# Hymba layer step: attention's value products in plain fp32, four heads to a PSUM bank

## Chip, cores and metric

The kernel runs on one core of a Trainium2 chip. The metric is device time in microseconds (us); lower is better. A core has five engines that each work through their instructions in order: TensorE (PE: matmuls, with weight loads, PEld, beside them), VectorE (DVE), ScalarE (ACT), GpSimd (POOL) and SyncE (SP), which here issues the DMAs. SBUF is the core's memory; PSUM's banks hold what PE writes.

## The reference, cut to what matters

One layer over a prompt of 512 tokens and 8 single sample tokens, `D_MODEL` 1024. The change concerns mixer B, dilated attention of 8 heads with 64 columns each, for the prompt:

```python
h = jnp.einsum('btd,de->bte', x, w_in)                      # 1024 -> 3600 columns
qa, ka, va, za, ga, qb, kb, vb, gb = jnp.split(h, split_points, axis=-1)
...                                                          # mixer A: gated linear attention -> o_a
# mixer B, for each (window, dilation) of (128,1), (512,4), (2048,16):
    logits = jnp.einsum('bqhd,bqjhd->bhqj', qf, kg) * scale + bias
    p = jnp.exp(logits - m);  s = jnp.sum(p, axis=-1, keepdims=True)
    outs.append(jnp.einsum('bhqj,bqjhd->bhqd', p, vg) / s)
out = (wts[0]*outs[0] + wts[1]*outs[1] + wts[2]*outs[2]) / (wts[0]+wts[1]+wts[2])
...
mix = jnp.concatenate([o_a * silu(ga), o_b * silu(gb)], axis=-1)
y = jnp.einsum('bte,ed->btd', mix, w_out)
x_new = layer_norm(DEEPNORM_ALPHA * x + y, ln_g, ln_b)
```

The keys and values of the prompt are outputs as well (`vw_p` in the kernel is the values' output, 512x512).

## The kernel before, in words

**Arithmetic.** All projections run in a reduced fp32 format (f32r) in three products: each operand is split into a high part, rounded to f32r by a cast, and a low part, the difference (`split`: a cast on ACT, a subtraction on DVE); then high by high, high by low and low by high are added in PSUM. Weights arrive by DMA in pieces (`raw0_gb0` is the first piece of group `gb0`), are split (`hi0_gb0`, `lo0_gb0`) and used by PE. The profile leaves the stage number out of such names: `hi_vb__1819` there is `hi1_vb1__1819` in the order of instructions.

**Who decides the order.** A small planner written in Python (`Plan`) runs while the program is built. Every piece of the layer is a generator, added with a priority (`add(weighted(h, pi), 30 + ...)`), that yields the next instruction, a need for a buffer, or a mark it waits for (`At`). The planner takes, again and again, the instruction that can start first by its own cost figures, and records it; on each engine the instructions then run in that order. A pair `copy(o, x)` may go to DVE or to ACT, whichever would end first by those figures; a `Batch` is recorded in one piece. Buffers come from pools with a fixed number of slots: `g` large SBUF tiles, `pt` probabilities, `t1` small temporaries, `ob` attention outputs, `r` raw weights; PSUM banks are of the kinds `d`, `s` and `t`. Since all instructions go out from one line of the planner, every line of the profile reads L359, and views go by the names of tiles.

**The stages on PE.** `dense` sets the sequence of the projections: `ka`, `za`, `qa`, `qb0` to `qb3`, `kb0` to `kb3`, `vb0`, `vb1`, `gb0` to `gb3`, `va0`, `va1`, `ga0` to `ga3`, then the output projection (`yf`, `y`) and the LayerNorm. All else is placed between their matmuls. The attention of the prompt runs in two halves `pi` of 256 queries: `scores` (two heads at a time, `ps_s`), `softmax` for each head and each tile of 128 queries, `weighted` for the product with the values, and `mix_b`, which multiplies by the gate. Beside it runs the attention of the samples over the cache: `past` and `qbc` come by DMA, POOL multiplies them, DVE reduces the product (`lt<-past`, eight times, named `past0` to `past7` in the order), and `l32` adds the samples' new key with a table `sel`.

**What the change touches.** `softmax` ends with a transpose on PE into a bank `ps_pt`, and from there a cast on ACT to the high part of the probabilities (`pt`, `pth`) and a subtraction on DVE to the low part (`pt`, `ptl`); one head of the first half has both parts in one slot, one of the second half takes two of the four. `vb_into` takes the values out of PSUM: for the first 256 tokens they come transposed and are turned back on PE (`ps_turn`), for the others they come in rows (`ps_vb`). Each piece is cast and subtracted into `vhl`, where a head's 64 high columns and 64 low ones stand side by side, and copied once more into a small tile (`raw` of `turn`, shown as `feat`, or `vb_raw`) from which a DMA stores it: eight stores of 128 KB. `weighted` multiplies for one head: the high probabilities by the 128 columns [high | low], the low ones by the 64 high columns:

```python
yield T.matmul(pv[:, o], vk, pth[:, k, o], start=k == 0, stop=False, ...)
yield T.matmul(pv[:64, o], vk[:, :64], ptl[:, k, o], start=False, stop=k == last, ...)
```

Partitions 64 to 127 of the bank are then copied by ACT (`pvl`, a slot of `t1`), and DVE adds the copy to partitions 0 to 63 into `obT`. These are 96 matmuls over both halves.

Of the kernel before, what the change touches and what calls it, by code (L numbers as in the profile page):

```python
# [11 lines left out]
F32 = mybir.dt.float32  # L12
# [46 lines left out]
    g=27,  # L59
# [304 lines left out]
def trunk(ctx: ExitStack, tc: tile.TileContext, xT, xp, xs, state, ck, cv, w_in, wab, gnorm,  # L364
# [44 lines left out]
    def copy(o, x):  # L409
        return V.tensor_copy(o, x), S.copy(o, x)  # L410
# [42 lines left out]
    class Group:  # L453
# [227 lines left out]
    def dense():  # L681
# [36 lines left out]
        for i in range(4):  # L718
            yield from make(f"kp{i}", Need("g", f"kp{i}", [P, 2, 512], F32R), 2)
            yield from feature(groups[f"kb{i}"], parts("k", k_s, i, 1.0))  # L720
        for i in range(2):
            for u in range(2):
                yield from make(f"vhl{i}{u}", Need("g", f"vhl{i}{u}", [P, 2, 4, 2, 64], F32R))
            yield from token(groups[f"vb{i}"], *vb_into(i))
# [343 lines left out]
    def vb_into(i):  # L1068
        def parts_of(o, x):
            yield S.copy(o[..., 0, :], x)  # L1070
            yield V.tensor_tensor(o[..., 1, :], x, o[..., 0, :].bitcast(F32), op=ALU.subtract)

        def evac_f(ps, f):
# [11 lines left out]
        def evac(ps, t):  # L1085
            yield from parts_of(B[f"vhl{i}1"][:, t - 2], ps.rearrange("p (h d) -> p h d", d=64))
            mark(f"vb{i}1")
            raw = yield Need("t1", "vb_raw", [P, GW])
            yield copy(raw, ps)
            free(ps)  # L1090
            yield D.dma_start(vw_p[t * P:t * P + P, i * GW:i * GW + GW], raw)
            free(raw)
        return evac_f, evac


# [46 lines left out]
    def softmax(h, q, ps_all, pr_all, cols):  # L1142
# [14 lines left out]
        if j == 0:  # L1157
            if pi:
                for x in "hl":
                    yield from make(f"pt{x}{h}{pi}", Need("pt", f"pt{x}{h}{pi}", [P, 4, 256], F32R))  # L1160
            else:
                B[f"pt{h}"] = yield Need("pt", f"pt{h}", [P, 2, 2, 256], F32R)
                B[f"pth{h}0"], B[f"ptl{h}0"] = B[f"pt{h}"][:, 0], B[f"pt{h}"][:, 1]
                mark(f"ptl{h}0")
        else:
            yield At(f"ptl{h}{pi}")
        pth, ptl = B[f"pth{h}{pi}"], B[f"ptl{h}{pi}"]
# [12 lines left out]
    def weighted(h, pi):  # L1180
        m, u = h // 2, (h % 2) * 64
        r = slice(u, u + 64)
        yield At(f"p{h}{pi}", 2)
        for i in range(pi + 1):
            yield At(f"vb{h // 4}{i}", 2)
        pth, ptl = B[f"pth{h}{pi}"], B[f"ptl{h}{pi}"]
        if h % 2 == 0:
            yield from make(f"obT{pi}{m}", Need("ob", f"obT{pi}{m}", [P, 256]))
        else:
            yield At(f"obT{pi}{m}")  # L1190
        pv = yield bank(("s", "t"), f"ps_pv{h}{pi}")
        last = 2 * pi + 1
        for k in range(last + 1):
            o = slice(P if k == last else 0, 256)
            vk = B[f"vhl{h // 4}{k // 2}"][:, k % 2, h % 4].rearrange("p u d -> p (u d)")
            yield T.matmul(pv[:, o], vk, pth[:, k, o], start=k == 0, stop=False, skip_group_check=True)
            yield T.matmul(pv[:64, o], vk[:, :64], ptl[:, k, o], start=False, stop=k == last, skip_group_check=True)
        free(*((pth, ptl) if pi else (pth,)))
        tmp = yield Need("t1", f"pvl{h}{pi}", [64, 256])
        yield S.copy(tmp, pv[64:, :256])  # L1200
        yield V.tensor_tensor(B[f"obT{pi}{m}"][r, :], pv[:64, :256], tmp, op=ALU.add)
        free(pv, tmp)
        mark(f"ob{pi}{m}")
        mark(f"ob{pi}")
        if B.setdefault(("pv_left", pi), 0) == HB - 1:
            if pi:
                free(*(B[f"vhl{i}{u}"] for i in range(2) for u in range(2)))
        B["pv_left", pi] += 1

# [173 lines left out]
    def mix_tiles(n, u):  # L1383
# [3 lines left out]
        else:  # L1387
            yield At(f"ob{u}0", 2)
# [23 lines left out]
    def mix_b(u, m):  # L1412
        yield At(f"ob{u}{m}", 2)
# [3 lines left out]
        yield V.tensor_tensor(gb, gb, B[f"obT{u}{m}"], op=ALU.mult)  # L1417
        free(B[f"obT{u}{m}"])
# [187 lines left out]
    add(keys_store(), 17.5)  # L1606
    for pi in range(2):
        for n in "ab":
            add(mix_tiles(n, pi), 13)
        for h in range(HB):  # L1610
# [3 lines left out]
            add(weighted(h, pi), 30 + 20 * pi / 100 + h / 100)  # L1614
# [100 lines left out]
```

## Time and profile before

| | |
|---|---|
| runs | 290.06, 289.52, 289.38 us; median 289.52 us |
| profiled execution, first to last instruction (span) | 286.8 us, 2.7 below the median of the runs; its own time outside the span is not recorded |
| granted TensorE clock | 0.994 |
| PE / weight loads | 275.0 us (96%) / 259.5 us (90%) |
| DVE / ACT / POOL | 225.7 us (79%) / 167.5 us (58%) / 55.9 us (19%) |
| DMA | 51.18 MB, mean 178 GB/s |
| value products on PE | first started at 104.5 us, last at 181.1 us, between `vb` and `va` |

Rows of groups give the line, the engine, the operation, the tile written and the tiles read, the shape, the count, the busy time with the mean of one, and behind the second bar the idle time of the engine just before, with what ended it. A row of the windows gives the length of the window and for PE, PEld, DVE, ACT and POOL the busy time with the number of instructions, then the granted clock, the share of the DMA engines' time and the rate. A row of the chain gives start, length and what ran; a row of the timeline adds in brackets the idle time before it and the releaser. Matmul ends are modelled; a matmul that waits inside the pipeline still counts as busy.

### The profile page before, as it was taken

Reading aid. Unit: us, or ns where it says so; the run is one execution under the profiler, and the core shown is the slowest. Engines: PE = TensorE matmul, PEld = TensorE weight load, DVE = VectorE, ACT = ScalarE, POOL = GpSimd, SP = SyncE. Lnnn points to the kernel's source line nnn. Section 1 sums busy time; section 2 is a strip of 40 time slices with the busy share of each in tenths; the row PEclk is TensorE's granted clock in tenths of the full one; section 3 lists DMA queues with packets and bytes.
Section 4 is the critical chain, followed back from the end, with each engine's and each line's share of the span. In section 5 each row is a group of like instructions: output and inputs, shape, how many; then the busy total and the mean of one; then the engine's idle time right before and its main releaser. Section 6 shows DMA issues by size and latency. Waiting matters only on the chain.

```text
span 286.8 us, 6896 instructions
## 1 busy us (share of the span) xinstructions
PE 275.0 (96%) x2636; PEld 259.5 (90%) x2636; DVE 225.7 (79%) x547; ACT 167.5 (58%) x478; POOL 55.9 (19%) x74
## 2 busy tenths in 40 slices
PE   8999999999999998999999999999999999999990
PEld 5899999998989998899989999999999999997880
DVE  3846897999889968988889997864888995339745
ACT  5757664554567777566869867526689774113201
POOL 4000001000782444401604444540000000000000
PEclk9999999999999999999999999999999999999997
DMA  7966522225866797648998987559754788741211
GB/s 209 269 191 195 147 75 75 75 78 167 296 201 222 196 287 230 175 130 243 274 201 188 239 227 219 149 149 228 221 95 148 230 297 252 111 151 73 78 75 73
DMA packets 58936, 51.18 MB, mean 178 GB/s; under 512 B 12555, under 2 KB 50197, under 8 KB 58903
## 3 DMA queue, kind: packets, MB, share of 16 engines
q1 hardware_dynamic: 58794, 50.66, 63.2%
q8 instruction: 21, 0.34, 0.5%
q14 instruction: 13, 0.10, 0.1%
q10 hardware_dynamic: 108, 0.07, 0.1%
HBM read 45.17 MB, written 6.03 MB: 179 GB/s over the span
## 4 chain that ended last, share of the span: by engine, by line
PE 71%; DVE 13%; DMA 8%; ACT 5%; issue 2%; SPq 1%; DVEq 0%; ACTq 0%
PE ps_qb L359 8%; PE ps_yf L359 8%; PE ps_y L359 8%; PE ps_ga L359 6%; PE ps_kb L359 4%; PE ps_qa L359 4%; PE ps_gb L359 4%; PE ps_va L359 4%; PE ps_ka L359 4%; DMA raw_gb__2152<-in_w_in_dram 3%; DMA out_dram<-feat 3%; PE ps_pt L359 2%; PE ps_va_f L359 2%; PE ps_l L359 2%; PE ps_s L359 2%; PE ps_pv L359 2%
## 5 line engine op out<-in xcount | busy, mean ns | idle before, releaser
L359 POOL TENSOR_TENSOR vv<-vv,pb 128x256 f32<-128x256 f32 x32 | 26.1, 846 | 45.5 <-DMA pb<-psd_s 39.8
L359 POOL TENSOR_TENSOR past<-past,qbc 128x256 f32<-128x256 f32 x32 | 25.6, 831 | 43.4 <-DMA past<-in_ck_dram 36.0
L359 ACT ACTIVATE pr<-pr,ms 128x128 f32<-128x128 f32 (+3 forms) x49 | 26.1, 546 | 5.8 <-DVE ms L359 5.2
L359 PE MATMUL ps_pt<-cf,pr 128*128 128x128 f32 x80 | 14.1, 280 | 1.4 <-DVE pt L359 1.0
L359 DVE CUSTOM_DVE_ANT_0 pr<-ps_s,strip 128x128 f32<-128x128 f32 (+3 forms) x32 | 14.3, 476 | 0.0
L359 PE MATMUL ps_ka<-xx,hi_ka 128*128 128x264 f32 (+1 forms) x64 | 13.5, 307 | 0.3 <-DVE xx L359 0.3
L359 ACT ACTIVATE sg<-sg 128x264 f32<-128x264 f32 (+1 forms) x32 | 13.4, 419 | 0.2
L359 PEld LDWEIGHTS ps_ka<-xx,hi_ka 128*128 128x128 f32 x64 | 11.0, 205 | 1.2 <-DVE xx L359 0.8
L359 DVE TENSOR_TENSOR ptl<-ps_pt,pth 128x384 fp32r<-128x384 f32 (+1 forms) x16 | 9.8, 617 | 2.8 <-ACT pth L359 2.8
L359 PEld LDWEIGHTS ps_pt<-cf,pr 128*128 128x128 f32 x80 | 9.0, 140 | 3.3 <-DVE pt L359 1.6
L359 ACT ACTIVATE d<-d 128x512 f32<-128x512 f32 x13 | 7.8, 637 | 6.7 <-DVE d L359 6.7
L359 ACT COPY feat_y<-ps_yf 128x256 f32<-128x256 f32 x8 | 3.0, 371 | 12.7 <-PE ps_yf L359 12.7
L359 ACT ACTIVATE rstd<-mv 128x1 f32<-128x1 f32 x4 | 0.7, 199 | 15.9 <-DVE mv L359 15.9
L359 POOL MEMSET att<- 64x512 f32 x2 | 1.0, 523 | 44.5 <-DVE ks L359 44.5
L359 ACT CAST pth<-ps_pt 128x384 fp32r<-128x384 f32 (+1 forms) x16 | 8.4, 534 | 2.2 <-PE ps_pt L359 2.0
L359 DVE TENSOR_REDUCE o_pv<-vv 128x4 f32<-128x1024 f32 x8 | 9.7, 1212 | 0.0
L359 DVE TENSOR_REDUCE lt<-past 128x16 f32<-128x1024 f32 x8 | 9.6, 1199 | 0.0
L359 PE MATMUL ps_ka<-xx,lo_ka 128*128 128x264 f32 (+1 forms) x32 | 9.4, 295 | 0.0
L359 DVE TENSOR_TENSOR obT<-ps_pv,pvl 64x256 f32<-64x256 f32 x16 | 6.6, 415 | 3.5 <-ACT pvl L359 3.3
L359 DVE TENSOR_TENSOR xx<-x_raw,xx 128x520 fp32r<-128x520 f32 (+2 forms) x9 | 5.8, 640 | 4.6 <-ACT xx L359 4.6
L359 ACT COPY pvl<-ps_pv 64x256 f32<-64x256 f32 x16 | 5.5, 370 | 6.1 <-PE ps_pv L359 5.3
L359 DVE TENSOR_TENSOR d<-b 128x1024 f32<-128x1024 f32 x7 | 8.5, 1218 | 0.0
(535 smaller groups left out, 1092.4 us busy)
## 6 DMA issues: line engine op xcount, KB each, us to landing
past<-in_ck_dram SPq DMA_DIRECT2D x8, 512.0 KB
vv<-in_cv_dram SPq DMA_DIRECT2D x8, 512.0 KB
pb<-psd_s SPq DMA_DIRECT2D x16, 256.0 KB
qbc<-qsd SPq DMA_DIRECT2D x8, 256.0 KB
strip<-tabr SPq DMA_DIRECT2D x8, 256.0 KB
y<-in_xp_dram SPq DMA_DIRECT2D x4, 512.0 KB
x_raw<-in_xT_dram SPq DMA_DIRECT2D x7, 260.0 KB
out_dram<-y SPq DMA_DIRECT2D x3, 512.0 KB
```

Of the source, the lines that this page charges most:

```text
L359: getattr(eng.eng, op.fn)(*op.args, **op.kw)
```

## The change

The probabilities and the values are no longer split. `softmax` copies the transposed probabilities once (DVE or ACT) as fp32. `vb_into` copies the values once, into two tiles `v0` and `v1` of 128 x 2 x 512 (two `g` slots instead of four, and `g` has 25 slots instead of 27), without the second copy; `values_store` stores each of the two tiles by one DMA of 512 KB when both column groups are in. `weighted` now works for a group of four heads: heads 0 and 2 of the group write partitions 0 to 63 of one bank, heads 1 and 3 partitions 64 to 127; heads 0 and 1 take the first 256 columns, 2 and 3 the last 256. Its plain fp32 matmuls, 8 for the first half of queries and 16 for the second (48 in all), are one batch in which the partition halves alternate, and one copy of 128x512 brings the bank to `obT`. It waits for the probabilities of all four heads, which hold the four `pt` slots until then.

```diff
-    g=27,
+    g=25,
...
-                tags += ("sv",) * (plan.marks["sample"] == 2) + ("pt",) * (plan.marks["ob1"] == HB) + ("g",)
+                tags += ("sv",) * (plan.marks["sample"] == 2) + ("pt",) * (plan.marks["ob1"] == 4) + ("g",)
...
     def vb_into(i):
-        def parts_of(o, x):
-            yield S.copy(o[..., 0, :], x)
-            yield V.tensor_tensor(o[..., 1, :], x, o[..., 0, :].bitcast(F32), op=ALU.subtract)
...
             ps, raw = yield from turn(ps)
-            yield from parts_of(B[f"vhl{i}0"][:, :, 2 * f:2 * f + 2], ps[:, :GW].rearrange("p (t h d) -> p t h d", t=2, d=64))
+            free(raw)
+            yield copy(B["v0"][:, :, c], ps[:, :GW].rearrange("p (t c) -> p t c", t=2))
+            free(ps)
             mark(f"vb{i}0")
-            yield copy(raw, ps[:, :GW])
+
+        def evac(ps, t):
+            yield copy(B["v1"][:, t - 2, i * GW:i * GW + GW], ps)
             free(ps)
-            yield D.dma_start(vw_p[:GW, c].rearrange("(t p) c -> p t c", p=P), raw.rearrange("p (t c) -> p t c", t=2))
-            free(raw)
...
+    def values_store(u):
+        for i in range(2):
+            yield At(f"vb{i}{u}", 2)
+        yield D.dma_start(vw_p[u * GW:u * GW + GW, :].rearrange("(t p) c -> p t c", p=P), B[f"v{u}"])
...
-        ptv = pt[:, :n].rearrange("p (k t) -> p k t", t=P)
-        yield S.copy(pth[:, :q + 1, qs], ptv)
-        yield V.tensor_tensor(ptl[:, :q + 1, qs], ptv, pth[:, :q + 1, qs].bitcast(F32), op=ALU.subtract)
+        yield copy(B[f"pt{h}{pi}"][:, :q + 1, qs], pt[:, :n].rearrange("p (k t) -> p k t", t=P))
...
-    def weighted(h, pi):
+    def weighted(g, pi):
+        hs = range(4 * g, 4 * g + 4)
+        for h in hs:
+            yield At(f"p{h}{pi}", 2)
+        for u in range(pi + 1):
+            yield At(f"vb{g}{u}", 2)
+        yield from make(f"obT{pi}{g}", Need("ob", f"obT{pi}{g}", [P, 2, 256]), 2)
+        pv = yield bank(("s", "t"), f"ps_pv{g}{pi}")
         last = 2 * pi + 1
+        pts = [B[f"pt{h}{pi}"] for h in hs]
+        every = [(k, h) for k in range(last + 1) for h in range(4)]
+        yield Batch(T.matmul(pv[h % 2 * 64:h % 2 * 64 + 64, h // 2 * GW + (P if k == last else 0):h // 2 * GW + GW],
+                             B[f"v{k // 2}"][:, k % 2, (4 * g + h) * 64:(4 * g + h) * 64 + 64], pts[h][:, k, P if k == last else 0:],
+                             start=k == 0 and h < 2, stop=k == last, skip_group_check=True) for k, h in every)
+        free(*pts)
+        yield copy(B[f"obT{pi}{g}"].rearrange("p m t -> p (m t)"), pv)
+        free(pv)
...
+    for u in range(2):
+        add(values_store(u), 17.5)
...
-            add(weighted(h, pi), 30 + 20 * pi / 100 + h / 100)
+            if h % 4 == 3:
+                add(weighted(h // 4, pi), 30 + 20 * pi / 100 + h / 100)
```

The planner is given other instructions and so records another order. Three places matter later; a name like `pt40` is head 4, query tile 0, and the number behind it is the buffer.

PE, at the first products, in the middle of the projection `vb0`; before, `ps_pv00` is head 0, half 0:

```order
L359 MATMUL ps_pv00_1727<-pt0_1262,vhl00_1578 128x256
L359 MATMUL ps_pv00_1727<-pt0_1262,vhl00_1578 64x256
L359 MATMUL ps_pv10_1728<-pt1_1294,vhl00_1578 128x256
L359 MATMUL ps_pv10_1728<-pt1_1294,vhl00_1578 64x256
L359 MATMUL ps_vb0_2_1679<-lo1_vb0__1408,xx6_240 128x256
L359 MATMUL ps_vb0_2_1679<-hi1_vb0__1407,xx6_241 128x256
L359 MATMUL ps_vb0_2_1679<-hi1_vb0__1407,xx6_240 128x256
L359 MATMUL ps_vb0_2_1679<-lo1_vb0__1408,xx6_240 128x256
L359 MATMUL ps_pv00_1727<-pt0_1262,vhl00_1578 128x128
L359 MATMUL ps_pv00_1727<-pt0_1262,vhl00_1578 64x128
```

The same place now; ten matmuls of `vb0` stand between the turning of the value tile and the first of these rows:

```order
L359 MATMUL ps_vb0_2_1672<-hi1_vb0__1403,xx6_240 128x256
L359 MATMUL ps_vb0_2_1672<-lo1_vb0__1404,xx6_240 128x256
L359 MATMUL ps_pv00_1709<-pt00_1262,v0_1572 64x256
L359 MATMUL ps_pv00_1709<-pt10_1294,v0_1572 64x256
L359 MATMUL ps_pv00_1709<-pt20_1439,v0_1572 64x256
L359 MATMUL ps_pv00_1709<-pt30_1473,v0_1572 64x256
L359 MATMUL ps_pv00_1709<-pt00_1262,v0_1572 64x128
L359 MATMUL ps_pv00_1709<-pt10_1294,v0_1572 64x128
L359 MATMUL ps_pv00_1709<-pt20_1439,v0_1572 64x128
L359 MATMUL ps_pv00_1709<-pt30_1473,v0_1572 64x128
L359 MATMUL ps_pt40_1729<-cf_66,pr40_1405 128x128
```

The products of four heads now stand together, and the transposes of head 4 come behind them.

DVE, at the second half of the split of weight group `vb1` (`lo1_vb1`), before:

```order
L359 TENSOR_REDUCE lt_82<-past5_1576 128x2x8
L359 TENSOR_TENSOR pt4_1749<-ps_pt41_1779,pt4_1749 128x2x128
L359 TENSOR_TENSOR pt5_1754<-ps_pt50_1791,pt5_1754 128x128
L359 TENSOR_TENSOR lo1_vb1__1820<-raw1_vb1__1496,hi1_vb1__1819 128x512
L359 TENSOR_TENSOR vhl01_1579<-ps_vb0_3_1771,vhl01_1579 128x4x64
L359 TENSOR_TENSOR l32_1722<-ln_new_1721,sel_1677 32x64
L359 TENSOR_TENSOR obT00_1726<-ps_pv10_1728,pvl10_1753 64x256
L359 TENSOR_TENSOR pt5_1754<-ps_pt51_1812,pt5_1754 128x2x128
L359 TENSOR_TENSOR pt6_1761<-ps_pt60_1824,pt6_1761 128x128
L359 COPY vb_raw_1840<-ps_vb0_3_1771 128x256
L359 TENSOR_TENSOR lo1_vb1__1820<-raw1_vb1__1496,hi1_vb1__1819 128x512
```

The same place now:

```order
L359 COPY pt40_1728<-ps_pt40_1729 128x128
L359 TENSOR_REDUCE lt_82<-past5_1558 128x2x8
L359 TENSOR_TENSOR l32_1704<-ln_new_1703,sel_1670 32x64
L359 TENSOR_REDUCE lt_82<-past6_1584 128x2x8
L359 TENSOR_TENSOR lo1_vb1__1803<-raw1_vb1__1482,hi1_vb1__1802 128x512 x2
L359 COPY cts_1791<-cts_raw_1789 66x258
L359 TENSOR_TENSOR lo0_gb0__1825<-raw0_gb0__1647,hi0_gb0__1824 128x1024
```

Before, `l32` stood between the two halves of the split, and the reduction of `past6` behind both; now both stand ahead of the split.

SP, the DMA issues at the same stage, before:

```order
L359 DMA past5_1576<-in_ck_dram 128x1024
L359 DMA raw0_gb0__1613<-in_w_in_dram 128x8x128
L359 DMA strip11_1633<-tabr_87 128x1x512
L359 DMA strip21_1642<-tabr_87 128x1x512
L359 DMA qbc6_1650<-qsd_89 128x512
L359 DMA past6_1662<-in_ck_dram 128x1024
L359 DMA out_5_dram<-feat_1627 128x2x128
L359 DMA sel_1677<-in_c_f_dram 64x224
```

and now:

```order
L359 DMA past5_1558<-in_ck_dram 128x1024
L359 DMA qbc6_1582<-qsd_89 128x512
L359 DMA past6_1584<-in_ck_dram 128x1024
L359 DMA strip11_1610<-tabr_87 128x1x512
L359 DMA strip21_1621<-tabr_87 128x1x512
L359 DMA raw0_gb0__1647<-in_w_in_dram 128x8x128
L359 DMA sel_1670<-in_c_f_dram 64x224
```

`raw0_gb0` has moved behind `past6` and the strips; the store of a feature is gone, and `sel` still comes last.

More of the change, by code (lines that the diff above doesn't have):

```diff
@@ L720, in dense @@
             yield from feature(groups[f"kb{i}"], parts("k", k_s, i, 1.0))
+        for u in range(2):
+            yield from make(f"v{u}", Need("g", f"v{u}", [P, 2, 512]))
         for i in range(2):
[L722 to L723 removed]
             yield from token(groups[f"vb{i}"], *vb_into(i))
@@ L1157, in softmax @@
         if j == 0:
[L1158 to L1164, printed above, removed]
-        else:
-            yield At(f"ptl{h}{pi}")
-        pth, ptl = B[f"pth{h}{pi}"], B[f"ptl{h}{pi}"]
+            yield from make(f"pt{h}{pi}", Need("pt", f"pt{h}{pi}", [P, 2 * pi + 2, 256]))
+        else:
+            yield At(f"pt{h}{pi}")
         pt = yield bank("t", f"ps_pt{h}{q}")
@@ L1178, in softmax @@
             mark("scores")
-    def weighted(h, pi):
[L1181 to L1191, printed above, removed]
-        last = 2 * pi + 1
[L1193 to L1208, printed above, removed]
@@ new lines, in weighted @@
+    def weighted(g, pi):
[6 more added lines that the diff above has]
+        pv = yield bank(("s", "t"), f"ps_pv{g}{pi}")
+        last = 2 * pi + 1
+        pts = [B[f"pt{h}{pi}"] for h in hs]
[6 more added lines that the diff above has]
+        free(pv)
+        for m in (2 * g, 2 * g + 1):
+            mark(f"ob{pi}{m}")
+            mark(f"ob{pi}")
+        if plan.marks[f"ob{pi}"] == 4 and pi:
+            free(B["v0"], B["v1"])
```

16 lines of the change are left out of this document (5 added, 11 removed).

## Prediction

> **What bounds the kernel now.** I read the page's busy shares and its chain of waits first.
>
> ```profile
> PE 275.0 (96%) x2636; PEld 259.5 (90%) x2636; DVE 225.7 (79%) x547; ACT 167.5 (58%) x478; POOL 55.9 (19%) x74
> PE 71%; DVE 13%; DMA 8%; ACT 5%; issue 2%; SPq 1%; DVEq 0%; ACTq 0%
> ```
>
> TensorE (PE) is busy for 96% of a span of 286.8 us, so all other engines together can lose it only the remaining 12 us and what is hidden in stretched matmuls. The change takes work from DVE and ACT; such work is worth something only where PE waits for it. Next the stages, by windows of 10 us (PE, PEld, DVE, ACT, POOL, then the granted clock, the DMA share and GB/s):
>
> ```profile
> 110.00:120.00 10.00, 8.65 (x67) 7.39 (x66) 9.21 (x20) 5.46 (x16) 6.92 (x8) 1.00 0.70 212
> 120.00:130.00 10.00, 10.00 (x87) 9.55 (x86) 8.53 (x28) 7.61 (x23) 0.00 (x0) 1.00 0.45 141
> 130.00:140.00 10.00, 10.00 (x86) 9.68 (x85) 9.21 (x26) 7.38 (x19) 2.86 (x4) 1.00 1.00 233
> 140.00:150.00 10.00, 9.74 (x84) 8.97 (x83) 8.40 (x16) 7.03 (x16) 3.06 (x4) 1.00 1.00 242
> 150.00:160.00 10.00, 9.94 (x86) 9.76 (x85) 9.94 (x28) 8.67 (x24) 3.94 (x5) 1.00 0.92 202
> 160.00:170.00 10.00, 9.96 (x83) 9.18 (x83) 9.93 (x25) 6.70 (x19) 5.67 (x8) 1.00 0.91 251
> 170.00:180.00 10.00, 9.88 (x83) 9.38 (x82) 8.30 (x19) 7.80 (x23) 3.16 (x4) 1.00 0.76 204
> ```
>
> A full window holds 87 matmuls. One stretch falls far short: 110 to 120 has 67, with PE idle 1.35 us and the rest lost in matmuls that wait inside. From 130 to 180 the windows lack 1, 3, 1, 4 and 4. The clock is 1.00 throughout, so none of this is the throttle. The chain, in order of time, names what stood in the way (start, us, what), and the timelines give the detail (start, us, engine, operation; in brackets the idle time before it and its releaser):
>
> ```profile
> 102.77 8.52 DMA out_dram<-feat
> 111.31 0.37 ACT pvl L359
> 111.68 0.52 ACT hi_vb__1819 L359
> 124.53 1.77 PE ps_pv L359 x16
> 148.66 1.01 PE ps_pv L359 x8
> 150.21 0.83 PE ps_pv L359 x8
> 209.11 11.71 PE ps_ga L359 x96
> 111.58 0.32 DVE L359 TENSOR_TENSOR l<-ln_new,sel 32x64 f32<-32x64 f32 x1 [0.43 <-DMA sel<-in_c_f_dram]
> 113.50 0.96 DVE L359 TENSOR_TENSOR lo_vb__1820<-raw_vb__1496,hi_vb__1819 128x512 fp32r<-128x512 f32 x1
> 114.51 0.39 PE L359 MATMUL ps_vb_f<-xx,lo_vb__1820 128*128 128x264 f32 x1 [0.61 <-DVE lo_vb__1820 L359]
> 117.34 1.20 DVE L359 TENSOR_REDUCE lt<-past 128x16 f32<-128x1024 f32 x1
> ```
>
> A store of a value feature holds a small buffer for 8.52 us; ScalarE's `pvl` copy waits for that buffer, the next weight split `hi_vb` stands behind it, its lower part `lo_vb` comes late on DVE, and PE waits. That is the one place where the work removed is the bound.
>
> **The change part by part.** First the evacuations that go: the groups of lines, keeping shapes apart where I need it (count | busy us, mean ns), and the value tile's own rows (ns min/median/max).
>
> ```profile
> L359 DVE TENSOR_TENSOR ptl<-ps_pt,pth 128x384 fp32r<-128x384 f32 (+1 forms) x16 | 9.8, 617 | 2.8 <-ACT pth L359 2.8
> L359 ACT CAST pth<-ps_pt 128x512 fp32r<-128x512 f32 x8 | 4.7, 589 | 1.7 <-PE ps_pt L359 1.6
> L359 ACT CAST pth<-ps_pt 128x384 fp32r<-128x384 f32 x8 | 3.8, 478 | 0.5 <-PE ps_pt L359 0.4
> L359 DVE TENSOR_TENSOR obT<-ps_pv,pvl 64x256 f32<-64x256 f32 x16 | 6.6, 415 | 3.5 <-ACT pvl L359 3.3
> L359 ACT COPY pvl<-ps_pv 64x256 f32<-64x256 f32 x16 | 5.5, 370 | 6.1 <-PE ps_pv L359 5.3 <-DMA out_dram<-feat 0.6
> L359 DVE TENSOR_TENSOR pt<-ps_pt,pt 128x128 fp32r<-128x128 f32 (+1 forms) x16 | 5.2, 344 | 0.6 <-ACT pt L359 0.6
> L359 ACT CAST pt<-ps_pt x16: 242/318/376, 80.6 to 117.8; 128x128 fp32r<-128x128 f32 x8, 128x256 fp32r<-128x256 f32 x8
> L359 ACT CAST vhl<-ps_turn x4: 348/365/378, 100.8 to 122.9; 128x256 fp32r<-128x256 f32 x4
> L359 DVE TENSOR_TENSOR vhl<-ps_turn,vhl x4: 403/412/426, 101.5 to 123.5; 128x256 fp32r<-128x256 f32 x4
> L359 ACT CAST vhl<-ps_vb x4: 373/375/378, 107.3 to 131.2; 128x256 fp32r<-128x256 f32 x4
> L359 DVE TENSOR_TENSOR vhl<-ps_vb,vhl x4: 418/424/425, 107.8 to 132.4; 128x256 fp32r<-128x256 f32 x4
> ```
>
> Probabilities: DVE 9.8 + 5.2, ACT 4.7 + 3.8 + 16 x 0.318 = 13.6. Product sums: DVE 6.6, ACT 5.5. Values: 4 x (0.365 + 0.412 + 0.375 + 0.424) = 6.3. Together 47.0 us of evacuation. Added by the prices of the like ACT casts: 32 probability copies, 13.6; eight value copies of 256 columns, 8 x 0.37 = 3.0; four bank copies of 128x512, 4 x 0.589 = 2.4; 19.0 in all. So 28 us of DVE and ACT time go, a little more with the raw value copies, which I leave out. On the path this counts only as follows.
>
> Term 1, the products on PE. They cost 2 x 1.77 for the first two heads' runs of 16 and eight runs of 8 at 0.83 to 1.01: 10.2 to 11.6, say 10.5. The new form, fp32 of 128x64 on alternating column halves, is not in the attention of before, but the state update of the other mixer has it:
>
> ```profile
> 198.11 0.41 PE L359 MATMUL ps_ga<-xx,hi_ga__2974 128*128 128x264 f32 x2
> 198.45 1.97 PE L359 MATMUL ps_kv<-va,kt 128*64 128x128 f32 x32
> 200.35 0.39 PE L359 MATMUL ps_ga<-xx,lo_ga__2975 128*128 128x264 f32 x1
> ```
>
> These are 16 fp32 matmuls, each recorded as two. A dense matmul follows the one before it by 11.71 / 96 = 0.122, so the pair at 198.11 shows 0.41 - 0.12 = 0.29 from start to end of one; taking that off the run of 32, one record needs (1.97 - 0.29) / 31 = 54 ns per 128 columns. The new products are 32 matmuls of 256 columns and 16 of 128, or 2 x (32 x 2 + 16) = 160 such units: 8.7 us. Then the way in and out: the next dense matmul was due at 198.11 + 2 x 0.122 = 198.35; it came at 200.35 and ran 0.10 longer than 0.29, an interruption of 2.10 where 32 x 54 ns is 1.73. The 0.37 left over, for four groups, makes 1.5. In all 10.2. Ends: 8.7 without any such price, and 160 / 32 x 2.10 = 10.5 with the whole interruption scaled. Against 10.5 that is -1.8 to 0; I take 0, since a batch of 8 or 16 no longer lets dense work in between. The Trainium skill's page "TensorEngine Tiling (Array Packing)", Key Properties, says that a change of tiling mode drains TensorE. By that rule the old products, which change between 128 and 64 columns at every matmul, would pay it some 32 times both ways, 32 x 0.37 = 11.8 by the leftover above, more than all that they take, and the change would win most of that. The trace disagrees: 0.83 for 8 such matmuls is 0.10 each with no room for a drain, so the sum goes by the rows.
>
> Term 2, the hole of 110 to 120: 20 matmuls short x 0.122 = 2.4 us. `pvl` and its wait are gone, so `hi_vb` no longer stands behind the store. But DVE's order changes just there. In the rows of DVE shown with the change, `l32`, which needs the small table `sel`, and the reduction of `past6` now stand ahead of both halves of `lo1_vb1`, the weight split that PE needs; before, one half stood ahead of both. If `sel` lands as before, at 111.58, the first half is done at 111.58 + 0.32 + 1.20 + 0.69 = 113.8 (0.69 is my estimate from the 0.96 of two overlapping rows, and 0.96 changes it by 0.3). PE reached its first upper-part matmul of that half at about 112.2 to 112.4, as the split `hi_vb` ended at 111.68 + 0.52. So a hole of 1.4 us is left of 2.4: -1.0, with ends 0 and -2.4.
>
> Term 3, 130 to 180: 13 matmuls short x 0.122 = 1.6. From 150 to 170 DVE is at 9.94 and 9.93 and loses subtractions and sums there; these windows and the next lack 9 of the 13. From 130 to 150 the DMA share is 1.00, the transfers set the pace, and nothing is won. 9 x 0.122 = 1.1, so I take -1.0, ends 0 and -1.6.
>
> Term 4, new waits. A product batch now needs the transposed probabilities of four heads and frees its four buffers, the whole pool, only together. The rows of PE show the first such place: the next head's transposes `ps_pt40` stand right behind the batch. Queued behind a waiting batch on PE is all dense work. Ahead of that batch ten dense matmuls, 1.2 us, follow the turning of the value tile on which its last copy waits, and a copy takes 0.37 to 0.59; that covers it unless DVE or ACT lag by more, and then the wait is theirs in full. I take +0.6, half a copy's 0.3 for each of two of the four batches, ends 0 and 2.0 (0.5 for each of four). The other mixer's stage from 198 on keeps its work and only shifts; the output projection at the end is untouched. The value stores move from eight transfers to two larger ones, costed at nothing: the last value row starts at 131.2, and 155 us of work behind it hide the stores; a longer queue for the weights would cost what it delays them, which case C holds.
>
> Sum: 0 - 1.0 - 1.0 + 0.6 = -1.4. The profiled span of 286.8 becomes 285.4; the median of the runs, 289.52, lies 2.7 above that span, so 288.1.
>
> **The rivals.** A, slower: `sel` lands late. In the rows of SP, `sel` stands behind `raw0_gb0` and `past6` before and after, but `raw0_gb0` now comes last of them, right ahead of `sel`, and its buffer comes free only when DVE is through an earlier weight split, which stands behind more softmax work than before. If `sel` lands at 114, the split is ready at 114 + 2.2 = 116.2, a hole of 4.0 against 2.4: +1.6, with terms 3 and 4 (+0.6 - 0.7, DVE being late) +1.5, so 291.0. It decides from about 112.6, where the hole is as large as before; each later microsecond costs one. For it: DVE did wait 0.43 for `sel`. Against it: the same bytes were queued ahead. 0.20.
>
> B, slower by far: the two column halves don't overlap at 256 columns, each matmul then takes twice the time. Term 1's 8.7 doubles: 288.1 + 8.7 = 296.8. It decides as soon as a batch of 16 takes over 2 us. Against it: the 54 ns per record of the same form. 0.05. The Trainium skill's page "FP8 and Floating Point Precision", TensorE Precision Notes, counts four passes through the array for true FP32. At a dense f32r matmul's 0.122 a pass, the products would take (32 + 16 / 2) x 4 x 0.122 = 19.5, about this rival's size, and the 16 of `ps_kv` 3.9; its row shows 1.97.
>
> C, nothing moves. The DMA share is 1.00 from 130 to 150, and PE's order is fixed when the program is built: time that DVE has to spare there is waited out at the next transfer. Terms 2 and 3 shrink to -0.3 each, and term 4 takes them back: 289.5. For it: even at DVE's 9.94 PE lost only 0.06 openly. 0.22.
>
> **How the numbers follow.** My forecast case has 0.53, A 0.20, B 0.05, C 0.22. About 0.3%, 0.87 us, is what a measurement of this kernel can tell from no change; 288.1 is 1.4 below. So faster 0.53, same 0.22, slower 0.25. Low end: term 2 full, term 3 full, term 1 at -0.5: 289.5 - 2.4 - 1.6 - 0.5 = 285.0. High end: A with 0.4 of a further microsecond, 291.4; B and the tail of A are left out.
>
> **What would show it.** Right: the products' four batches add up to 10 us in the timeline, the window of 110 to 120 has 75 matmuls or more, no `pvl` in the chain, and DVE's busy time down by 15 to 25 us (it loses 9.8 + 5.2 + 6.6 + 3.3 = 24.9 and takes a part of the 19 added) with the span little changed. Term 2 is wrong if DVE's `l32` waits for `sel` past 112.6, or if the hole is gone. Term 4 is wrong if PE's products show idle time behind a copy of `pt`. The forecast falls if the span moves by over 3 us, or if a stretch outside 100 to 190 changes its own length by over 1 us.

## The result, and the profile after

The changed kernel takes 287.5 us in the median of 17 runs, the kernel before 289.38 on the same chip; the ratio is 0.9949 (95% interval 0.9927 to 0.997). The forecast was 288.1, faster. The profiled span is 285.4 us, as forecast, but two parts of the way there were not. In every run whose span is on record the time lies 1.7 to 2.0 us above the span, so the profiled span of before, 286.8, belongs to an execution of about 288.7, some 0.7 below the median; differences between the two profiles come out about that much too small. The busy shares and the chain of waits of the changed kernel:

```profile
PE 272.6 (95%) x2636; PEld 254.8 (89%) x2636; DVE 208.4 (73%) x496; ACT 161.2 (56%) x453; POOL 59.4 (21%) x74
PE 67%; DVE 14%; ACT 9%; DMA 6%; issue 2%; SPq 0%; DVEq 0%; ACTq 0%
```

DVE lost 17.3 us of work and ACT 6.3; PE's busy time fell by 2.4 and the span by 1.4. The windows of the attention, columns as before:

```profile
110.00:120.00 10.00, 9.93 (x80) 8.96 (x79) 8.74 (x22) 7.26 (x20) 4.63 (x4) 1.00 0.53 159
120.00:130.00 10.00, 9.90 (x85) 8.31 (x84) 3.22 (x12) 4.68 (x12) 0.00 (x0) 1.00 0.69 195
130.00:140.00 10.00, 10.00 (x88) 8.99 (x89) 9.74 (x25) 8.74 (x21) 6.81 (x7) 1.00 1.07 225
140.00:150.00 10.00, 10.00 (x91) 8.82 (x87) 8.79 (x23) 8.82 (x22) 1.13 (x2) 1.00 0.99 232
150.00:160.00 10.00, 10.00 (x90) 8.79 (x89) 8.70 (x21) 6.59 (x19) 5.28 (x6) 1.00 0.93 207
160.00:170.00 10.00, 10.00 (x85) 10.00 (x86) 6.84 (x16) 6.41 (x16) 5.07 (x7) 1.00 1.01 257
170.00:180.00 10.00, 10.00 (x86) 10.00 (x85) 5.69 (x8) 4.18 (x14) 3.21 (x4) 1.00 0.72 216
```

110 to 120 holds 80 matmuls instead of 67, and PE no longer stands idle anywhere from 130 to 180, in spite of a DMA share of 0.93 to 1.07 up to 170. The four product batches in the chain:

```profile
105.17 1.45 PE ps_pv L359 x16
123.93 1.45 PE ps_pv L359 x16
138.69 3.18 PE ps_pv L359 x32
156.71 3.18 PE ps_pv L359 x32
```

For a balance over the whole program I added up in both traces, for every matmul, the time from its start to the next one's start, and grouped that by the tile written. It is PE's whole time, waits included:

| tiles | before, us | after, us | difference |
|---|---|---|---|
| warm-up and `ka`, the first loads | 17.03 | 17.44 | +0.4 |
| `za` to `qb`, with `l` | 46.75 | 46.71 | 0.0 |
| products `pv` | 10.09 | 9.26 | -0.8 |
| `kb`, `kt`, `s`, `pt`, `turn`, `vb_f`, `vb`, `sl`, `pn`, `rows` | 72.25 | 71.08 | -1.2 |
| `gb`, `va_f`, `va` | 48.96 | 47.45 | -1.5 |
| `ga`, `kv`, `oa`, `og`, `oat`, `ort` | 34.34 | 34.74 | +0.4 |
| `yf` | 24.03 | 25.56 | +1.5 |
| the rest, to the last matmul | 24.33 | 24.36 | 0.0 |

By the end of `va` PE is 3.5 us ahead, less 0.4 for the first loads; then it gives 1.9 back. Two open waits make up 1.6 of that: 0.4 us at `ps_oa`, and 1.2 at `ps_ort`, the transpose of the samples' result in mixer A (the balance books this one under `yf`, the tile of the matmul before it). Changed kernel, timelines of PE, ACT and DVE:

```profile
230.81 0.30 PE L359 MATMUL ps_ort<-cf,o_r 128*128 128x128 f32 x1 [1.21 <-DVE o_r L359]
226.28 0.62 ACT L359 CAST hi_wo__3414<-raw_wo__3342 128x512 fp32r<-128x512 f32 x1 [0.29 <-DMA raw_wo__3342<-in_w_out_dram]
227.64 0.20 ACT L359 ACTIVATE rs_s<-rs_s 128x1 f32<-128x1 f32 x1
229.53 0.74 DVE L359 SCALAR_TENSOR_TENSOR ga<-ps_oat,gn,ga 128x512 f32<-128x512 f32 x1
230.19 0.15 DVE L359 SCALAR_TENSOR_TENSOR rs_s<-newton,ss_s 128x1 f32<-128x1 f32 x1
230.37 0.29 DVE L359 TENSOR_SCALAR o_r<-o_r,rs_s 128x128 f32<-128x128 f32 x1
```

On ACT both casts of an output weight stand ahead of its part of `rs_s`, and the first waits for its DMA. That part is done at 227.84. Four small steps on DVE complete `rs_s` at 230.34, with a weight split and two gate products `ga` before and among them; then come `o_r` and PE's transpose. From ACT's part to the start of `o_r` it was 2.5 us in the kernel before as well (224.87 to 227.38). What differs is PE's order: there PE reached the transpose 2.5 us after ACT's part, here 1.8. The row of `ps_ort` before:

```profile
227.71 0.33 PE L359 MATMUL ps_ort<-cf,o_r 128*128 128x128 f32 x1 [0.30 <-DVE o_r L359]
```

### The profile page after: what moved, and what is told of

Its sections match the earlier page's. It is cut to its first block, busy times and chain, and to the rows that moved or that the text cites. A ratio compares the mean times of both kernels' runs of the same rounds, so it can differ in the third digit from the quotient of the medians.

```text
span 285.4 us, 6811 instructions
## 1 busy us (share of the span) xinstructions
PE 272.6 (95%) x2636; PEld 254.8 (89%) x2636; DVE 208.4 (73%) x496; ACT 161.2 (56%) x453; POOL 59.4 (21%) x74
## 4 chain that ended last, share of the span: by engine, by line
PE 67%; DVE 14%; ACT 9%; DMA 6%; issue 2%; SPq 0%; DVEq 0%; ACTq 0%
PE ps_gb L359 8%; PE ps_qb L359 8%; PE ps_y L359 8%; PE ps_yf L359 7%; PE ps_va_f L359 4%; PE ps_qa L359 4%; PE ps_va L359 4%; PE ps_pv L359 3%; PE ps_ka L359 3%; PE ps_vb L359 3%; DVE pr L359 3%; PE ps_pt L359 2%; DMA x_raw<-in_xT_dram 2%; PE ps_l L359 2%; PE ps_s L359 2%
## 5 line engine op out<-in xcount | busy, mean ns | idle before, releaser
L359 POOL TENSOR_TENSOR vv<-vv,pb 128x256 f32<-128x256 f32 x32 | 29.1, 942 | 41.2 <-DMA pb<-psd_s 38.8
L359 POOL TENSOR_TENSOR past<-past,qbc 128x256 f32<-128x256 f32 x32 | 26.1, 848 | 32.5 <-DMA past<-in_ck_dram 28.0
L359 ACT ACTIVATE pr<-pr,ms 128x256 f32<-128x256 f32 (+3 forms) x51 | 27.2, 548 | 7.7 <-DVE ms L359 7.4
L359 DVE CUSTOM_DVE_ANT_0 pr<-ps_s,strip 128x128 f32<-128x128 f32 (+3 forms) x32 | 14.1, 477 | 2.3 <-PE ps_s L359 1.8
L359 PE MATMUL ps_ka<-xx,hi_ka 128*128 128x264 f32 (+1 forms) x64 | 12.5, 292 | 1.9 <-ACT xx L359 1.2
L359 ACT ACTIVATE sg<-sg 128x264 f32<-128x264 f32 (+1 forms) x32 | 13.4, 417 | 0.3
L359 PE MATMUL ps_pt<-cf,pr 128*128 128x128 f32 x80 | 13.3, 274 | 0.0
L359 PEld LDWEIGHTS ps_ka<-xx,hi_ka 128*128 128x128 f32 x64 | 10.1, 188 | 2.7 <-ACT xx L359 1.4
L359 POOL MEMSET att<- 64x512 f32 x2 | 1.0, 522 | 54.5 <-DVE ks L359 54.5
L359 ACT ACTIVATE d<-d 128x512 f32<-128x512 f32 x13 | 7.8, 637 | 6.7 <-DVE d L359 6.7
L359 DVE TENSOR_REDUCE o_pv<-vv 128x4 f32<-128x1024 f32 x8 | 9.7, 1214 | 1.9 <-POOL vv L359 1.9
L359 ACT COPY pt<-ps_pt 128x256 f32<-128x256 f32 (+3 forms) x23 | 9.8, 427 | 2.3 <-PE ps_pt L359 2.1
L359 ACT COPY feat_y<-ps_yf 128x256 f32<-128x256 f32 x8 | 3.0, 374 | 12.8 <-PE ps_yf L359 12.8
L359 PEld LDWEIGHTS ps_pt<-cf,pr 128*128 128x128 f32 x80 | 9.3, 140 | 0.5 <-issue 0.5
L359 ACT ACTIVATE rstd<-mv 128x1 f32<-128x1 f32 x4 | 0.7, 199 | 16.0 <-DVE mv L359 16.0
L359 DVE TENSOR_REDUCE lt<-past 128x16 f32<-128x1024 f32 x8 | 9.6, 1202 | 0.0
L359 PE MATMUL ps_pv<-pt,v 128*64 128x256 f32 (+1 forms) x96 | 9.5, 348 | 0.0
L359 PE MATMUL ps_ka<-xx,lo_ka 128*128 128x264 f32 (+1 forms) x32 | 9.1, 283 | 0.0
L359 DVE TENSOR_TENSOR xx<-x_raw,xx 128x520 fp32r<-128x520 f32 (+2 forms) x9 | 5.8, 640 | 4.5 <-ACT xx L359 4.4
L359 PEld LDWEIGHTS ps_pv<-pt,v 128*64 128x64 f32 x96 | 6.3, 137 | 3.0 <-issue 0.4
L359 DVE TENSOR_TENSOR d<-b 128x1024 f32<-128x1024 f32 x7 | 8.5, 1217 | 0.0
L359 PE MATMUL ps_s<-kp,qh 64*128 64x128 f32 (+3 forms) x64 | 8.3, 345 | 0.0
```

The source lines that it names most:

```text
L359: getattr(eng.eng, op.fn)(*op.args, **op.kw)
```

## The experiments

All ratios are to the kernel before, measured on the same chip beside it; the changed kernel stands at 0.9949.

### What the four heads' products cost

`serial_halves`: the order inside a batch is changed when it is recorded, after the planning, so that every engine's order stays otherwise. (In rows of edited kernels the line that records instructions has another number than L359.)

```diff
-        every matmul of the batch in the order (k, head 0 1 2 3)
+        for u in range(2):  every matmul with head % 2 == u, in the order of k
```

> The changed kernel with every engine's order kept except inside the four product batches: all matmuls on the first column half come first, then those on the second. Theory (two matmuls on different halves run at once, 52 ns per record of 128 columns): the products' 8.3 us of matmuls double, the batches of 16 and 32 records take about 2.6 and 6.1 us instead of 1.45 and 3.18, and the time is 287.5 + 8 = 295.5. Rival: the price does not come from the halves, and the time stays within 0.5 of 287.5.

Measured 294.75 us in two runs, ratio 1.0191 (1.0125 to 1.0256), 7.2 above the changed kernel. Its chain:

```profile
124.80 2.37 PE ps_pv L326 x14
140.47 5.82 PE ps_pv L326 x30
161.09 5.82 PE ps_pv L326 x30
```

The batch of 32 takes 5.82 (the chain names 30 of its 32 records) instead of 3.18, and in the balance the products go from 9.26 to 16.37. The starts of the records show why: at 256 columns each step takes 0.216 us in both traces, but with alternating halves two records start in it, 7 ns apart, and with the halves in turn only one. Two matmuls on different column halves do run at once, and that is worth 7.1 us here. Rival B is refuted.

### Was the hole of 110 to 120 the small buffer?

`no_pvl` (the kernel before, its order kept):

```diff
-        yield S.copy(tmp, pv[64:, :256])                       # recorded
-        yield V.tensor_tensor(obT[r, :], pv[:64, :256], tmp, op=ALU.add)
+        # the copy is planned but not recorded
+        yield V.tensor_copy(obT[r, :], pv[:64, :256])          # planned as the sum
```

> The kernel before with every engine's order kept, without the 16 copies pvl; DVE copies the bank's first half instead of adding both (the product with the values' low part is left out of the result). Theory (the hole of 110 to 120 is the copy that waited for a store's buffer): the hole of 2.4 shrinks, 289.4 - 1.0 to 2.4 = 287.0 to 288.4. Rival: the table sel and DVE keep PE late there, 289.4 - 0 to 0.5.

Measured 290.12, ratio 1.0015 (0.998 to 1.0049): nothing. Its window and PE's longest wait in it (what waited, us in total, times, longest):

```profile
110.00:120.00 10.00, 8.57 (x67) 7.31 (x66) 9.96 (x21) 4.91 (x15) 7.05 (x8) 1.00 0.56 166
PE ps_vb_f L361 <- DVE lo_vb__1818 L361: 0.9, 1, 0.9
```

The same 67 matmuls, with DVE at 9.96 of 10. The chain of before was true for that execution (the store did hold the buffer for 8.52 us). Taking the waiting copy away lets ACT's second half of `hi_vb` start at 110.08 instead of 111.58. But DVE, full by then, ends `lo_vb` only 0.4 us earlier, at 114.03 instead of 114.46, and PE, which is 0.5 us earlier itself, waits for it as before. In the kernel before itself, PE's longest waits from 60 to 200 us are these:

```profile
PE ps_pt L359 <- DVE pt L359: 1.0, 3, 0.4
PE ps_vb_f L359 <- DVE lo_vb__1820 L359: 0.6, 1, 0.6
```

The larger wait is that of the transposes for their bank `ps_pt`, which comes free only when DVE has subtracted the low part; 0.7 us of it lie between 110 and 120.

`t1_seven` (the kernel before, one more small buffer, planned anew):

```diff
-    t1=6, ob=4,
+    t1=7, ob=4,
...                  # two small constants share memory with dead ones
```

> The kernel before with seven small buffers (t1) instead of six, so that a copy need not wait for a feature's store; two small constants share memory with dead ones for it. Theory (the hole of 110 to 120 comes from the copy pvl that waited 8.5 us for a store): the hole shrinks and the time falls by 1.0 to 2.4, 287.0 to 288.4. Rival: DVE's own work and the table sel make PE late there anyway, the time stays at 289.4 within 0.5.

Measured 287.63, ratio 0.9927 (0.989 to 0.9964). This looked like the theory's proof; after `no_pvl` it isn't one. The edit also made the planner draw another order for all engines, and the last group below shows how much that alone moves.

`no_subtract` (the kernel before, its order kept):

```diff
-        yield V.tensor_tensor(ptl[...], ptv, pth[...], op=ALU.subtract)      # recorded
-            yield T.matmul(pv[:64, o], vk[:, :64], ptl[:, k, o], ...)
+        # the subtraction is planned but not recorded
+            yield T.matmul(pv[:64, o], vk[:, :64], pth[:, k, o], ...)        # planned with ptl
```

> The kernel before with every engine's order kept, without the 32 subtractions that make the probabilities' low part; the low products read the high part instead, so PE does the same work (the low part is left out of the result). Theory 1: with 15 us less on DVE PE's waits shrink, 289.4 - 1.0 to 2.5 = 286.9 to 288.4. Rival 3: PE waits for other things, 289.4 - 0 to 0.5.

Measured 286.9, ratio 0.9917 (0.9886 to 0.9947), 2.4 us:

```profile
110.00:120.00 10.00, 9.58 (x78) 8.69 (x77) 9.15 (x19) 6.92 (x20) 7.11 (x8) 1.00 0.74 217
PE ps_vb_f L361 <- DVE lo_vb__1810 L361: 0.4, 1, 0.4
```

The window goes from 67 to 78, though ACT's copy still waits for the store (0.65 us at 111.56), and the waits of the transposes for the subtraction are gone. So in the order of before, the subtractions on DVE made the hole, by their time and by the bank that they held, not the wait on ACT.

### Putting the work back

`dve_back` (the changed kernel, its order kept):

```diff
         yield copy(B[f"pt{h}{pi}"][:, :q + 1, qs], ptv)
+        # recorded right behind it, unknown to the planner:
+        nc.vector.tensor_tensor(pt, ptv, pt, op=ALU.max)
```

> The changed kernel with every engine's order kept, and behind each of the 32 probability copies one more VectorE instruction that reads the bank and the copy and writes the same values back, of the shapes of the former subtractions (some 15 us of DVE in all); the products wait for it as they did before. Theory 1 (the gain comes from evacuation work that no longer delays PE): the late splits and the waits return, 287.5 + 2.0 to 3.0 = 289.5 to 290.5. Rival 3 (that work was off the path, and the gain is the new order and the shorter products): 287.5 + 0 to 0.5.

Measured 297.24, ratio 1.0295 (1.0246 to 1.0344), 9.7 us above the changed kernel for 15.6 us of DVE. Its added instructions (ns min/median/max) and two windows:

```profile
L1164 DVE TENSOR_TENSOR pt<-ps_pt,pt x32: 281/486/691, 80.4 to 165.2; 128x128 f32<-128x128 f32 x8, 128x256 f32<-128x256 f32 x8, 128x384 f32<-128x384 f32 x8, 128x512 f32<-128x512 f32 x8
140.00:150.00 10.00, 8.21 (x71) 6.98 (x72) 9.72 (x24) 6.31 (x16) 2.86 (x3) 1.00 0.70 190
150.00:160.00 10.00, 8.62 (x69) 7.47 (x67) 9.70 (x23) 7.34 (x19) 3.18 (x4) 1.00 1.10 180
```

Three to five times what was expected. Not all of it is DVE's load: the added instructions stand in DVE's order right behind copies that ACT may make, and DVE waited 4.8 us for those (nine times). The rest I put down to an order that was made without this work and has no place for it, which is not shown separately.

`work_replanned` (the same work, known to the planner):

```diff
-        yield copy(B[f"pt{h}{pi}"][:, :q + 1, qs], ptv)
+        yield S.copy(B[f"pt{h}{pi}"][:, :q + 1, qs], ptv)
+        yield V.tensor_tensor(B[f"pt{h}{pi}"][:, :q + 1, qs], ptv, B[f"pt{h}{pi}"][:, :q + 1, qs], op=ALU.max)
```

> The changed kernel with each probability copy as an ACT copy and a VectorE instruction of the former subtraction's shape behind it, both known to the planner, which orders anew. Theory 1: 15 us of DVE work cost what they cost in the kernel before, where leaving them out won 2.4: 287.5 + 2.4 = 289.9 (289 to 291). Rival: with the kept order they cost 9.8, and it is the work itself that costs it: 297.

Measured 287.44, ratio 0.9915 (0.988 to 0.9951): with DVE back at 219.5 us it is as fast as the changed kernel, and both theories of the expectation miss.

```profile
PE 273.9 (96%) x2636; PEld 255.0 (89%) x2636; DVE 219.5 (77%) x522; ACT 162.1 (57%) x459; POOL 59.0 (21%) x74
```

`stores_back` (the changed kernel with the former value stores):

```diff
             yield copy(B["v1"][:, t - 2, i * GW:i * GW + GW], ps)
+            raw = yield Need("t1", "vb_raw", [P, GW])
+            yield copy(raw, ps)
+            yield D.dma_start(vw_p[t * P:t * P + P, i * GW:i * GW + GW], raw)
...          # the same for the turned half; no values_store
```

> The changed kernel with the values stored as before: eight more copies of 256 columns into small buffers and eight stores of 128 KB instead of two of 512 KB. Theory 1 (the gain comes from the probability and product evacuations and the product itself): 3.0 us of copies come back, off PE's path for the most part, so 287.5 + 0.5 (0 to 1.0). Rival 2 (what held the kernel before was the small buffers waiting for those stores): most of the gain goes, 289.0 to 289.5.

Measured 287.25, ratio 0.9912 (0.987 to 0.9954): not slower, and rival 2 falls. The fewer stores are worth nothing that can be seen. Its waits on PE lie elsewhere again:

```profile
PE ps_pt L359 <- ACT pr L359: 1.6, 1, 1.6
PE ps_ort L359 <- DVE o_r L359: 0.3, 1, 0.3
```

### The time given back

`gla_after` and `gla_before`, the same edit in both kernels:

```diff
         for i in range(2):                 # two halves of the samples' state
-            load s4, load v4; update; store
+            load s4, load v4
+        for i in range(2):
+            update; store
```

> The changed kernel, in which the state update of the samples (mixer A) issues the loads of both halves before the first update instead of after the first store; up to the end of the va projection every engine's order is as in the changed kernel. Theory 1: the changed kernel wins about 3.6 us by the end of va and gives about 2 back afterwards, because its order interleaves the samples' updates with the evacuation of ps_oa, so that the second half loads late, ps_og comes late and PE waits 1.2 us at ps_ort. Then the hole at ps_ort goes and the time is 287.5 - 1.2 = 286.3 (285.8 to 286.8). Rival: ACT is full there (9.97 of 10 us) whatever the order, and the time stays at 287.5 within 0.3.

> The same edit in the kernel before. Theory 1: there PE waits only 0.3 us at ps_ort, so 289.4 becomes 289.1 at most, a gain of 0 to 0.4. Rival: the edit is worth as much here as in the changed kernel, about 1.2, and 288.2 would follow; then the give-back isn't the change's.

Measured 287.51, ratio 0.9933 (0.9903 to 0.9962), and 290.57, ratio 1.0039 (1.0004 to 1.0074): no gain in either kernel, so theory 1 misses for the changed one. The edit moves the changed kernel's transpose ten microseconds ahead, and the wait goes with it:

```profile
221.11 0.33 PE L359 MATMUL ps_ort<-cf,o_r 128*128 128x128 f32 x1 [1.02 <-DVE o_r L359]
```

The planner puts `ps_ort` where it reckons `o_r` to be ready, and that was 0.3 to 1.2 us too early in the orders seen so far.

`ort_later`: the order of the changed kernel with `ps_ort` some 15 matmuls later.

```diff
-        yield V.tensor_scalar(o_r, o_r, rs, None, op0=ALU.mult)
+        op = V.tensor_scalar(o_r, o_r, rs, None, op0=ALU.mult)
+        op.lag = 2500                      # added to its end in the planner's books
+        yield op
```

> The changed kernel, in which the planner is told that the samples' output o_r is ready 2.5 us later than it reckons; PE's order is kept but for ps_ort, which moves back by some 15 matmuls of the output projection (on DVE and ACT a few splits of output weights change places). Theory 4 (the 1.2 us of PE at ps_ort is a misjudged place in the order): the hole goes and the time is 287.5 - 1.0 = 286.5 (286.1 to 286.9). Rival: the transposes ps_oat behind it wait as long, and the time stays at 287.5 within 0.4.

Measured 288.73, ratio 0.995 (0.9923 to 0.9976): no gain. The wait at `ps_ort` is gone, and the next one behind it takes its place; and a wait that the changed kernel's own profile did not have stands first:

```profile
PE ps_vb_f L360 <- DVE lo_vb__1803 L360: 2.1, 1, 2.1
PE ps_oat L360 <- DVE ga L360: 0.9, 1, 0.9
```

That first wait lies in a stretch in which both kernels have the same order. DVE's timeline there, first the changed kernel, then this one:

```profile
111.19 0.21 DVE L359 TENSOR_TENSOR l<-ln_new,sel 32x64 f32<-32x64 f32 x1 [2.86 <-DMA sel<-in_c_f_dram]
112.47 1.27 DVE L359 TENSOR_TENSOR lo_vb__1803<-raw_vb__1482,hi_vb__1802 128x512 fp32r<-128x512 f32 x2
```

```profile
112.72 0.21 DVE L360 TENSOR_TENSOR l<-ln_new,sel 32x64 f32<-32x64 f32 x1 [4.86 <-DMA sel<-in_c_f_dram]
113.99 1.27 DVE L360 TENSOR_TENSOR lo_vb__1803<-raw_vb__1482,hi_vb__1802 128x512 fp32r<-128x512 f32 x2
110.00:120.00 10.00, 7.93 (x65) 7.19 (x64) 7.24 (x18) 5.88 (x16) 4.76 (x5) 1.00 0.52 140
```

`sel` landed 1.5 us later in this execution, and the window holds 15 matmuls fewer than in the changed kernel's, 1.8 us. So far this is rival A, in one execution and not in another. But rival A's reason, that `sel` is issued late behind `raw0_gb0` and its buffer, is not what happened. The issues on SP's queue, first the changed kernel, then this one:

```profile
102.03 2.27 SPq L359 DMA_DIRECT2D sel<-in_c_f_dram  x1
101.57 3.46 SPq L360 DMA_DIRECT2D sel<-in_c_f_dram  x1
```

The issue of `sel` began half a microsecond earlier, but took 1.2 us longer, and `sel` came later still. The time went after SP had reached it, and what held it there is open.

### How much is the order?

`after_610` and `before_610`: one cost in the planner's books, in both kernels; the work is the same.

```diff
-TO_PE, FROM_PE, OTHER, AFTER_DMA, WITHIN = 600.0, ...
+TO_PE, FROM_PE, OTHER, AFTER_DMA, WITHIN = 610.0, ...
```

> The changed kernel with one of the planner's costs changed by 10 ns (the delay before PE sees another engine's result, 600 to 610), so that it orders anew with the same work. If the gain of the change is its work and not a lucky order, 287.5 within 1.0. If it is the order, 289 or more.

> The kernel before with the same 10 ns. If its order was neither lucky nor unlucky, 289.4 within 1.0. If the kernel before was unlucky, 288 or less, and the gain of the change shrinks by as much.

Measured 289.12, ratio 0.9982 (0.9952 to 1.0013), and 295.14, ratio 1.0177 (1.0134 to 1.0219). Ten nanoseconds in a cost make the kernel before 5 us slower and take most of the changed kernel's gain, as far as intervals that overlap allow (0.9952 to 1.0013 against 0.9927 to 0.997). By the words of the first expectation that speaks for the order; the second had no place for a kernel that gets slower. PE's largest waits in `before_610` do not have one cause:

```profile
PE ps_oat L359 <- DVE ga L359: 1.4, 1, 1.4
PE ps_yf L359 <- ACT hi_wo__3696 L359: 1.4, 1, 1.4
PE ps_gb L359 <- DVE ms L359: 0.6, 1, 0.6
PE ps_rows L359 <- ACT vnt L359: 0.6, 1, 0.6
```

Over all orders drawn here, the kernels with the new product and a planned order lie at 0.9912, 0.9915, 0.9933, 0.9949, 0.995 and 0.9982, those with the old product at 0.9927, 1, 1.0039 and 1.0177. In each of the six the products take 9.26 us in the balance; in the four old ones 10.1 to 10.7.

The balance of these ten profiles, one execution each, tells a little more. (They hold seven orders of the attention: `gla_after` and `ort_later` have that of the changed kernel up to the end of `va`, and `gla_before` that of the kernel before.) The attention stretch (the rows of `pv`, of `kb` to `rows` and of `gb` to `va` together) takes 127.8 to 130.5 us with the new product and 131.3 to 133.0 with the old one: the two do not overlap. The stretch behind it (the rows of `ga` to `ort` and of `yf`) takes 58.4 to 60.8 with the new and 58.4 to 63.1 with the old; `stores_back` and `work_replanned`, at 58.4 and 58.6, give nothing back. So the loss after `va` goes with the order drawn, and not with the change alone, while some gain in the attention came with every order of the new product.

## Why the prediction was right, and where it was not

**Term 1, the products: 0 forecast, -0.8 measured.** The 54 ns for each unit hold. From its first start to the start of the next matmul a batch of 16 records, 24 units or 1.30 us, takes 1.45; one of 32, 56 units or 3.02, takes 3.18. To these 0.15 comes what the neighbours lose. PE around the last batch of the changed kernel:

```profile
156.43 0.28 PE L359 MATMUL ps_gb<-xx,hi_gb__2128 128*128 128x264 f32 x1
156.64 3.25 PE L359 MATMUL ps_pv<-pt,v 128*64 128x256 f32 x32
159.82 0.39 PE L359 MATMUL ps_gb<-xx,hi_gb__2128 128*128 128x264 f32 x1
160.04 0.28 PE L359 MATMUL ps_gb<-xx,lo_gb__2129 128*128 128x264 f32 x1
```

The dense matmul before and the one behind take 0.21 and 0.22 to the next start instead of 0.12. That makes 0.35 for going in and out, close to the 0.37 that `ps_kv` gave; the balance books the neighbours' part under `gb`. The other three batches have transposes behind them and lose less there. In the balance the new products took 9.3 instead of 10.2 and the old ones 10.1 instead of 10.5, and the difference of -0.3 between the two forecasts had been set to 0. (Where the prediction has the old products change their width "some 32 times both ways", they do it 48 times; its answer there stays the same.)

**Term 2, the hole: -1.0 forecast, -1.1 to -1.6 measured.** The window has 13 matmuls more, or -1.6; with the windows before and behind it, which lost two each, it is 252 for 243, or -1.1, and the balance has -1.2 for `kb` to `rows`. `sel` landed at 111.19 (111.58 forecast), and the reduction and the split followed at once. But the rest of the hole was not the forecast 1.4. PE at the split:

```profile
112.71 0.40 PE L359 MATMUL ps_vb_f<-xx,hi_vb__1802 128*128 128x264 f32 x2
113.19 0.39 PE L359 MATMUL ps_vb_f<-xx,lo_vb__1803 128*128 128x264 f32 x1
```

PE came later than the assumed 112.2 to 112.4: the matmul that needs the split was due at about 112.95 and started 0.24 late. What is left depends on when `sel` lands; in `ort_later` 1.5 us of delay cost 1.8. Wrong was the step before all this, the reading of the chain: the store, the buffer and `pvl` were not the bound (`no_pvl`, no gain), DVE's own subtractions were (`no_subtract`, 2.4 us). Both go in the change, so the sum did not notice; that was luck.

**Term 3, 130 to 180: -1.0 forecast, -1.5 measured** for `gb` and `va`. Even where the DMA share is 1.00, PE lost nothing, which I had not expected. That the removed work did this is not shown: with the order of before kept, `no_subtract` brings this row only from 48.96 to 48.67, and `after_610`, with the work of the changed kernel in another order, has 49.76, more than the kernel before.

**Term 4, the new waits: +0.6 forecast, none measured.** From 60 to 200 us PE waits openly in the changed kernel only here:

```profile
PE ps_kt L359 <- DVE kd L359: 0.3, 1, 0.3
PE ps_turn L359 <- ACT feat L359: 0.2, 1, 0.2
```

No batch waits for a fourth head, and no transpose for its buffers.

**Not forecast: +1.9 after `va`.** "The other mixer's stage from 198 on keeps its work and only shifts; the output projection at the end is untouched" was the wrong sentence. Both keep their work, but not their order, and the new order holds waits that the old one did not. One of the prediction's own signs of failure came true by it: `yf`, which runs from 227 us on, grew by 1.5 us, and a stretch outside 100 to 190 was not to change by over 1. The time came out all the same because this loss and the four terms' shortfall (-1.4 forecast, -3.1 by the end of `va`, first loads included) nearly cancel. That is luck, and not the mechanism.

**From the span to the median: 2.7 used, 1.7 to 2.0 on record.** With 1.9 the same span of 285.4 gives 287.3, nearer to the measured 287.5 than 288.1.

**Rival A** did not happen in the changed kernel's profile (`sel` at 111.19, before 112.6); a late `sel` and its price are real in `ort_later`, but without the late issue that rival A gives as the reason. **Rival B** is refuted. **Rival C**, that the transfers set the pace where the DMA share is 1.00 and DVE's spare time is waited out there, is refuted for the changed kernel: in these windows PE is busy for 10.00 of 10 us, with 88 and 91 matmuls.

**What stays open.** With the order kept, the evacuation work is worth 2.4 us (`no_subtract`) to 9.7 (`dve_back`, DVE's waits for ACT included); when the planner may order anew, putting 15 us of it back costs nothing that can be seen (`work_replanned`). Shown as the change's own are the 0.8 us of the products. Whether the rest of the 1.5 us is the removed work or a luckier order isn't settled: one cost moved by 10 ns shifts a kernel by up to 1.8%, more than the change. That the attention stretch was shorter in all four new orders than in all three old ones, and longest among the new ones in `work_replanned`, speaks for the work; but each profile is a single execution, and `sel` alone moves this stretch by 1.7 us between `ort_later` and the changed kernel. None of the variants beats the changed kernel beyond the intervals; `stores_back` has the lowest ratio, and its interval holds 0.9949.

## What to carry to other kernels

Where a planner or scheduler sets the order, compare several orders of the same work before a change of half a per cent is put down to its work; a cost moved by a trifle gives them cheaply. To learn what a piece of work costs, plan with it and leave it out when recording, or the other way round, so that nothing else moves. A chain of waits names what ended last in one execution; only taking that wait away shows whether something else stood right behind it.

## What had not been expected of the hardware

Two fp32 matmuls of 128x64 on different column halves overlap almost wholly when they alternate (9.26 us against 16.37 for the same 48). A change from dense work to such a batch and back costs about 0.35 us where dense matmuls stand on both sides: 0.15 inside the batch and 0.1 at each neighbour. A DMA of 56 KB that had the same place in the same order landed 1.5 us apart in two executions, at 111.19 and 112.72, although the later one's issue began earlier; its window lost 1.8 us, or 0.6% of the time.
